# A sum over rows on one core: the block of 17 rows per partition, numbered otherwise

## The chip, the cores and the metric

The kernel runs on one NeuronCore of a Trainium2 chip (trn2). The core has a matrix engine (PE, unused here), a vector engine (DVE), a scalar engine (ACT), a general engine (POOL), a queue engine (SP) that issues transfers, and 16 DMA engines that move data between the chip's memory (HBM) and the core's on-chip memory (SBUF, 128 partitions). The metric is the device time of one execution in microseconds; the median of three runs is given.

## The reference

```python
batch, seq, dim = 32, 512, 1024
x = np.random.randn(batch, seq, dim).astype(np.float32)
divisor = float(dim)

def reference(x, divisor):
    return (np.sum(x, axis=-1) / divisor).astype(np.float32)
```

16,384 rows of 1024 float32 (4 KB a row, 67.1 MB in all) are each summed and divided by 1024. The output is one float32 a row, 64 KB.

## The kernel before

The 16,384 rows are dealt to the 128 partitions, 128 rows (J) to each. They are not one consecutive block a partition but two parts. In the first part, of F = 17 rows per partition, partition p has the rows 17p to 17p + 16: a block of 17 x 4 KB = 68 KB, and the blocks of the 128 partitions follow each other in memory. The second part has W = 111 rows per partition, again one block each (444 KB), of which the first M = 95 are called main and the remaining L = 16 last. The DRAM patterns are `x_first`, `x_main` and `x_last`, and `o_first`, `o_main` and `o_last` for the results.

All loads go through three buffers `bulk0` to `bulk2` of 16 rows per partition, taken in turn. The list `loads` sets their order: 2 rows of the first part (`begin`), then six loads of the main part (five of 16 rows, one of 15), then the other 15 rows of the first part (`first`), then 10 and 4 rows of the last part. The last two rows of a partition come in two small transfers, `pa` (1536 elements) and `pb` (512).

All transfers are issued by SP, in the order in which they stand. The first three loads (line 114) need no wait; they are lifted into the program's first block, ahead of SP's part of the starting barrier, so that they are issued as the very first thing (`start_loads_at_once`). Each later load (line 141) waits until DVE, and where ACT had a share also ACT, has read the load three places before in the same buffer (semaphores `dve` and `act`) and that load has landed. Then SP issues `pa` and `pb` (lines 143, 144), waits for POOL and stores `res` (`o_main`, line 146), waits for POOL again and stores `res0` (`o_first`, line 148), waits for the last sums and stores `fin` (`o_last`, line 205), waits until the two earlier stores have landed, clears the semaphores and waits for the last landing.

DVE takes each load when it has landed. For the loads of the first and main parts it does one `reduce_sum` over all rows of the load that are its own (line 191): for the 2-row load both, for a 16-row load all 16, for the 15-row loads 11 and 9. ACT does the remaining 4 and 6 rows with one activation each that accumulates along the row (line 167). The last part is done row by row, by DVE (line 182, both halves of a row at once) and ACT. POOL scales `res` (line 155) and `res0` (line 159) by 1/1024; the last part is scaled as it is summed.

A transfer of 128 partitions is carried by all 16 DMA engines: in the packet records of the trace each load shows 128 packets, one a partition, and the semaphore that tells of its landing is raised 16 times. SP issues a transfer in some 0.33 to 0.44 us and goes on; the data move on their own.

Of the kernel before, what the change touches and what calls it, by code (L numbers as in the profile page):

```python
# [35 lines left out]
def kernel(  # L36
# [9 lines left out]
    N, D = xf.shape  # L46
    P = nc.NUM_PARTITIONS
    scale = 1.0 / float(divisor)
# [3 lines left out]
    F, L = 17, 16  # L52
    M = J - F - L
    W = M + L
    x_first = bass.AP(tensor=x.tensor, offset=0, ap=[[F * D, P], [D, F], [1, D]])
    x_main = bass.AP(tensor=x.tensor, offset=P * F * D, ap=[[W * D, P], [D, M], [1, D]])
    x_last = bass.AP(tensor=x.tensor, offset=P * F * D + M * D, ap=[[W * D, P], [D, L], [1, D]])
    o_first = bass.AP(tensor=out.tensor, offset=0, ap=[[F, P], [1, F]])
    o_main = bass.AP(tensor=out.tensor, offset=P * F, ap=[[W, P], [1, M]])
    o_last = bass.AP(tensor=out.tensor, offset=P * F + M, ap=[[W, P], [1, L]])  # L60

    def room(name, *shape):
        return nc.alloc_sbuf_tensor(name, [P, *shape], F32).ap()
# [9 lines left out]
    res0 = room("res0", F)  # L73
    res = room("res", M)
    fin = room("fin", L)
# [4 lines left out]
    loads = []  # L80
# [16 lines left out]
    first = [(15, 6)]  # L97
    last = [(10, 4), (4, 1)]
    assert sum(r for r, _ in begin + first) == F
    assert sum(r for r, _ in main) == M and sum(r for r, _ in last) == L - 2  # L100
    for part, src, dst, by in (
        (begin, x_first, res0, 1.0), (main, x_main, res, 1.0),
        (first, x_first[:, 2:], res0[:, 2:], 1.0), (last, x_last, fin, scale),
    ):
        j = 0
        for rows, on_act in part:
            t, s, slot = bulk[n % 3][:, :rows, :], in_bulk[n % 3], n
            n += 1
            loads.append((t, s, src[:, j : j + rows, :], on_act, dst[:, j : j + rows], by, slot))
            j += rows  # L110


# [9 lines left out]
    for k, (t, s, src, on_act, dst, by, slot) in enumerate(loads):  # L122
        rows = t.shape[1]
# [45 lines left out]
    for k, (t, s, src, on_act, dst, by, slot) in enumerate(loads):  # L169
        rows = t.shape[1]  # L170
# [76 lines left out]
```

## Time and profile before

| | |
|---|---|
| median of 3 runs | 160.36 us (160.34 to 160.55) |
| the profiled execution | 160.63 us |
| its span, first to last instruction | 159.3 us |
| DVE busy | 116.5 us (73%), 30 instructions |
| ACT busy | 18.5 us (12%), 33 instructions |
| POOL busy | 1.0 us (1%), 7 instructions |
| DMA | 67.18 MB in 2160 packets, 422 GB/s over the span |

The span is measured between the first and the last instruction; the device time has about 1.3 us more around it. Busy time of an engine does not count register, branch, semaphore and DMA-issuing instructions. The profile is one execution; the median is over other executions, without a profiler.

What each load waits for and when it lands, from the trace's semaphore records and the timeline:

| load | rows | issued at, us | landed at, us |
|---|---|---|---|
| first part (`begin`) | 2 | 0.00 | 4.80 |
| main 1 | 16 | 0.42 | 24.13 |
| main 2 | 16 | 0.89 | 43.52 |
| first part (`first`) | 15 | 99.45 | 137.84 |
| `pa` | 1.5 | 132.01 | 156.65 |
| `pb` | 0.5 | 132.49 | 157.30 |

The difference of a landing and an issue is not the time that a transfer takes alone: the transfers of SP's queue are carried one after the other, and a later one waits for those before it.

### The profile page before, as it was taken

What the parts mean: (1) busy time and instruction counts of PE and PEld (TensorE: products, weight loads), DVE (VectorE), ACT (ScalarE), POOL (GpSimd) and SP (SyncE); (2) the same over time, 40 slices, a digit from 0 to 9 for tenths busy, and PEclk for the clock granted to TensorE, in tenths of its full rate; (3) what the DMA queues carried; (4) which work ended last, traced back from release to release, by engine and by line L of the source; (5) the groups of instructions that cost most, each with busy time, mean ns of one, the idle gap of its engine ahead of it and who ended that gap; (6) DMA issues with size and microseconds to landing.
All of it is one profiled execution on the core that took longest, in us unless ns stands there. A gap on an engine that the chain in (4) does not pass through costs nothing.

```text
span 159.3 us, 140 instructions
## 1 busy us (share of the span) xinstructions
DVE 116.5 (73%) x30; ACT 18.5 (12%) x33; POOL 1.0 (1%) x7
## 2 busy tenths in 40 slices
DVE  0500009999499994999949999499989990399475
ACT  3000000000000000000000000000009100392384
POOL 0000000000000000000000000000000001000000
DMA  9996996996996997999969969988999799797993
GB/s 376 413 527 263 527 527 263 527 510 280 527 510 280 527 477 313 527 395 395 527 263 527 527 263 527 494 386 355 494 494 417 324 494 494 329 483 339 424 425 122
DMA packets 2160, 67.18 MB, mean 422 GB/s; under 512 B 624, under 2 KB 624, under 8 KB 880
## 3 DMA queue, kind: packets, MB, share of 16 engines
q1 hardware_dynamic: 2160, 67.18, 98.0%
HBM read 67.11 MB, written 0.07 MB: 422 GB/s over the span
## 4 chain that ended last, share of the span: by engine, by line
DMA 67%; DVE 29%; another core or an unknown queue 1%; ACT 1%; SPq 1%; issue 0%
DMA bulk<-in_x_dram 52%; DVE res L191 29%; DMA pa<-in_x_dram 15%; ACT junk L167 1%; SPq L114 1%; SPq L141 0%
## 5 line engine op out<-in xcount | busy, mean ns | idle before, releaser
L191 DVE TENSOR_REDUCE res<-bulk 128x16 f32<-128x16384 f32 (+3 forms) x8 | 110.0, 13753 | 37.6 <-DMA bulk<-in_x_dram 37.6
L167 ACT ACTIVATE junk<-bulk 128x1024 f32<-128x1024 f32 x15 | 15.2, 1011 | 136.2 <-DMA bulk<-in_x_dram 136.2
L182 DVE CUSTOM_DVE_ANT_0 bulk<-bulk 128x512 f32<-128x512 f32 x9 | 5.7, 690 | 3.4 <-DMA bulk<-in_x_dram 3.4
L167 ACT ACTIVATION_READ_ACCUMULATOR junk<-bulk 128x1 f32 x15 | 2.8, 187 | 0.0
L167 ACT ACT_TABLE_LOAD x1 | 1.3, 1283 | 2.4 <-PEq L117 2.4
L155 POOL TENSOR_SCALAR res<-res 128x95 f32<-128x95 f32 x1 | 0.5, 463 | 129.2 <-DVE res L191 129.2
L167 ACT ACTIVATE junk<-pa 128x1024 f32<-128x1024 f32 x1 | 1.0, 1027 | 0.7 <-DMA pa<-in_x_dram 0.7
L182 DVE DVE_READ_ACCUMULATOR2_ANT fin<- 128x1 f32 x10 | 0.8, 84 | 0.0
L182 DVE CUSTOM_DVE_ANT_0 pb<-pb 128x257 f32<-128x257 f32 x1 | 0.4, 429 | 0.2 <-DMA pb<-in_x_dram 0.2
L182 DVE CUSTOM_DVE_ANT_0 pa<-pa 128x256 f32<-128x256 f32 x1 | 0.4, 425 | 0.0
L159 POOL TENSOR_SCALAR res<-res 128x17 f32<-128x17 f32 x1 | 0.3, 265 | 15.6 <-DVE res L191 15.6
L167 ACT ACTIVATION_READ_ACCUMULATOR junk<-pa 128x1 f32 x1 | 0.2, 188 | 0.0
L151 POOL MEMSET pb<- 128x2 f32 x1 | 0.1, 100 | 2.0 <-POOLq L117 2.0
L228 POOL MEMSET const-uint8-127<- 128x1 uint8 x1 | 0.1, 102 | 0.0
L228 POOL MEMSET const-bfloat16-1.0<- 128x1 bf16 x1 | 0.1, 101 | 0.0
L228 POOL MEMSET const-float32-0.0<- 128x1 f32 x1 | 0.1, 98 | 0.2 <-issue 0.2
L228 POOL MEMSET const-float32-1.0<- 128x1 f32 x1 | 0.1, 98 | 0.0
L182 DVE DVE_READ_ACCUMULATOR2_ANT pb<- 128x1 f32 x1 | 0.1, 83 | 0.0
## 6 DMA issues: line engine op xcount, KB each, us to landing
bulk<-in_x_dram SPq DMA_DIRECT2D x2, 7680.0 KB, 39.0
bulk<-in_x_dram SPq DMA_DIRECT2D x1, 5120.0 KB, 31.1
bulk<-in_x_dram SPq DMA_DIRECT2D x1, 2048.0 KB, 23.1
bulk<-in_x_dram SPq DMA_DIRECT2D x1, 1024.0 KB, 4.8
pa<-in_x_dram SPq DMA_DIRECT2D x1, 768.0 KB, 24.6
pb<-in_x_dram SPq DMA_DIRECT2D x1, 256.0 KB, 24.8
bulk<-in_x_dram SPq DMA_DIRECT2D x5, 40.8
out_dram<-res SPq DMA_DIRECT2D x1, 47.5 KB, 24.6
```

Source lines behind the costliest of these rows:

```text
L114: i = nc.sync.dma_start(out=t, in_=src).then_inc(s, 16)
L151: nc.gpsimd.memset(pb[:, D - c :], 0.0).then_inc(pool)
L155: nc.gpsimd.tensor_scalar_mul(out=res, in0=res, scalar1=scale).then_inc(pool)
L159: nc.gpsimd.tensor_scalar_mul(out=res0, in0=res0, scalar1=scale).then_inc(pool)
L167: nc.scalar.activation(junk[a % len(junk)], src, COPY, scale=by, accum_out=dst).then_inc(count)
L182: return nc.vector.tensor_tensor_reduce(out=src[:, :h], in0=src[:, :h], in1=src[:, h:], scale=by, scalar=0.0, op0=ADD, op1=ADD, accum_out=dst,
L191: nc.vector.reduce_sum(out=dst[:, :m], in_=t[:, :m, :], axis=AX).then_inc(dve)
L228: nc = _bacc.Bacc("TRN2", target_bir_lowering=False, num_devices=1)
```

## The change

In the first part, partition p = 4a + b (a from 0 to 31, b from 0 to 3) no longer has block p but block a + 32b. The function `spread(step)` gives the two dimensions: 32 steps of one block, and inside each four steps of 32 blocks. `x_first` becomes a function of the first row and the number of rows, which builds the pattern of one load; `o_first` gets the same two dimensions, so that the results go to the rows that belong to the blocks. The list of loads is built with the row offset 2 in place of a slice. Nothing else changes: sizes, buffers, order, waits and the engines' work are as before. In the built program three transfers are touched: the 2-row load, the 15-row load and the store of `res0`; they now have three dimensions a side (32 x 4 x run in DRAM, 128 x 1 x run in SBUF), where all others have two. In the built program every transfer of two dimensions carries a mark named "precooked", and these three no longer do.

```diff
-    x_first = bass.AP(tensor=x.tensor, offset=0, ap=[[F * D, P], [D, F], [1, D]])
+    def spread(step):
+
+        return [[step, P // 4], [P // 4 * step, 4]]
+
+    def x_first(j, rows):
+        return bass.AP(tensor=x.tensor, offset=j * D, ap=[*spread(F * D), [1, rows * D]])
+
     x_main = bass.AP(tensor=x.tensor, offset=P * F * D, ap=[[W * D, P], [D, M], [1, D]])
...
-    o_first = bass.AP(tensor=out.tensor, offset=0, ap=[[F, P], [1, F]])
+    o_first = bass.AP(tensor=out.tensor, offset=0, ap=[*spread(F), [1, F]])
...
-        (first, x_first[:, 2:], res0[:, 2:], 1.0), (last, x_last, fin, scale),
+        (first, x_first, res0, 1.0), (last, x_last, fin, scale),
     ):
-        j = 0
+        j = 2 if part is first else 0
         for rows, on_act in part:
             t, s, slot = bulk[n % 3][:, :rows, :], in_bulk[n % 3], n
             n += 1
-            loads.append((t, s, src[:, j : j + rows, :], on_act, dst[:, j : j + rows], by, slot))
+            loads.append((t, s, src(j, rows) if src is x_first else src[:, j : j + rows, :], on_act, dst[:, j : j + rows], by, slot))
             j += rows
```

## The prediction

> **What bounds the kernel now.** I read four views: the page's DMA lines, the chain of waits in order of time, the groups of instructions, and the start and end of the timeline. First the page's DMA slices and its queue:
>
> ```profile
> DMA  9996996996996997999969969988999799797993
> ...
> q1 hardware_dynamic: 2160, 67.18, 98.0%
> HBM read 67.11 MB, written 0.07 MB: 422 GB/s over the span
> ```
>
> The 16 DMA engines carry 67.18 MB and are at work for 98.0% of the 159.3 us span. The 6s in the row of digits are an effect of where packets of 64 KB begin, not idle time: a packet is booked whole in the slice in which it starts. In the packet records (16 engines; each carries 8 packets of a 128-partition load) the 640 packets of 65,536 B have a median of 2418 ns and a maximum of 2434, and the 256 of 61,440 B have 2267 and 2302. Both are 27.1 B/ns an engine, and the next packet of an engine starts 3 to 4 ns before the one ahead of it ends. So from the first load to the last there is nothing to win or hide: whatever an engine is late by at its start, it is late by at its end.
>
> The chain in order of time (start, length, what) says the same:
>
> ```profile
> 0.00 0.38 SPq L114
> ...
> 0.89 42.63 DMA bulk<-in_x_dram
> ...
> 80.14 39.56 DMA bulk<-in_x_dram
> ...
> 132.01 24.64 DMA pa<-in_x_dram
> ...
> 156.68 1.15 ACT junk L167 x2
> ```
>
> It opens with SP's issue of the first load at L114 and closes with the `pa` transfer, one activation and the last store. The DVE pieces that it names in between are not what limits: the groups show that DVE waited for data before its reductions:
>
> ```profile
> L191 DVE TENSOR_REDUCE res<-bulk 128x16 f32<-128x16384 f32 (+3 forms) x8 | 110.0, 13753 | 37.6 <-DMA bulk<-in_x_dram 37.6
> L167 ACT ACTIVATE junk<-bulk 128x1024 f32<-128x1024 f32 x15 | 15.2, 1011 | 136.2 <-DMA bulk<-in_x_dram 136.2
> ```
>
> Columns: busy us and mean ns of one, then idle us and what ended it. 37.6 us of idle time on DVE, all ended by loads, is slack of the compute side. Last the timeline, its start and end (start, us, what):
>
> ```profile
> 0.00 1.32 SPq L114 DMA_DIRECT2D bulk<-in_x_dram  x3
> ...
> 4.83 2.29 DVE L191 TENSOR_REDUCE res<-bulk 128x2 f32<-128x2048 f32 x1 [4.83 <-DMA bulk<-in_x_dram]
> ...
> 148.06 0.34 SPq L148 DMA_DIRECT2D out_dram<-res  x1
> ...
> 157.85 0.33 SPq L205 DMA_DIRECT2D out_dram<-fin  x1
> ```
>
> Between the first issue and full pace lies the only soft stretch. In the packet records the first of the 128 packets of 8 KB starts at 1.00 us, 0.62 us after the 0.375 us issue has ended. An 8 KB packet at pace takes 309 ns, but most of the first 16 to start take 411 to 816 ns, and one takes 1014. The excess of all 128 over 309 ns, divided by 16, is 0.45 us an engine. The first 64 KB packet starts at 3.92 us on the earliest engine and at 4.53 on the latest; the one next to it starts at 4.25. That spread stays: the last 61,440 B packets start between 134.56 and 135.25, with the second latest at 134.85. The end waits for the latest engine.
>
> **The change part by part.** Three transfers change, all by one pattern: the load of 2 rows (first at L114), the load of 15 rows (at L141, the eighth in the list) and the store of `res0` (L148). Their bytes, order, waits and increments stay, and so do all instructions of DVE, ACT and POOL. What differs is which block of 68 KB a partition gets and that the instruction has three dimensions where it had two: 32 x 4 x run in DRAM, 128 x 1 x run in SBUF. The built program also marks every two-dimensional transfer "precooked" and leaves that mark off these three.
>
> 1. Issue of the first load. L114 holds SP for 375 ns now, and the data start follows it. No row shows an issue with three dimensions. Nearest rows: issues on an otherwise idle SP take 327 to 343 ns, those behind another 424 to 440, all of two dimensions. Lower bound of the extra: 0 (nothing is taken away that would shorten it). Upper bound: one more whole issue, 0.43 us. The record grows by half (three pairs a side for two), which on 375 ns is 0.19; with the lost mark as a second reason I take the middle, 0.21 us. It lies on the path in full: no packet moves before it.
>
> 2. The second and third issue shift by the same 0.21 us. They are hidden: the first load keeps the engines until 3.9 us, and the third issue ends at 1.32. Were that cover gone, it would be the same 0.21 that item 1 counts, not one more.
>
> 3. Issue of the 15-row load. It starts at 99.45 us, and its first packet moves at 100.57 + 8 x 2.267 = 118.7. So 19 us hide even a doubled issue. Behind it on SP are the loads of 10 and 4 rows, which wait for later reductions anyway. Cost 0.
>
> 4. Store of `res0`. Issued at 148.06, landed at 157.67 (last of its 16 semaphore steps), because its 68 B packets (12 ns each) lie behind the loads in the rings. SP waits for it only after the last store's issue at 157.85 has ended at 158.18, and the last store itself lands at 159.27. A longer issue is hidden by the 9.6 us in the ring. The 68 B pieces now go 2,176 B apart where four were adjacent; 1.6 us of cover remain. Cost 0; if all 8 pieces of an engine took ten times 12 ns, 0.96 us, still covered.
>
> 5. The addresses. Neighbouring engines (four partitions each) started 4 x 68 = 272 KB apart and now start 68 KB apart; the four partitions of an engine are 2,176 KB apart where they were 68. At full pace the pitch has not mattered here: the main load (4 x 444 = 1,776 KB between engines) and the 15-row load (272 KB) both run at 27.1 B/ns. For the 15-row load I take 0; the upper bound is that its packets all become like the slowest seen, 8 x (2302 - 2267) = 0.28 us an engine, the lower bound 0, as 2267 is the floor. For the start-up excess I take 0 too, since the rows show no link to the pitch, but both ends are open: below, the latest engine becomes as early as today's earliest, 3.92 - 4.53 = -0.61; above, the excess of 0.45 doubles, +0.45.
>
> One rule speaks to item 5. The Trainium skill, "DMA: Bandwidth & Descriptors", section "Latency and other measured facts", says that a row pitch of 2 MiB between partitions gave 164 GB/s where 512 KiB gave 207, and that a few KiB of padding bring the rate back. Read against this change, 2,176 KB would cost nothing by its padding clause (128 KiB over 2 MiB), and by its first clause 8.9 MB at 164/207 of the pace, an estimate of some 5.5 us more. No row here has such a pitch.
>
> Sum: 0.21 + 0 + 0 + 0 + 0 = +0.21 us. The profiled execution took 160.63 us, 159.30 of it span and 1.33 around it; with the change 159.51 and 160.84. The median of the three runs shown is 160.36, 0.27 under the profiled one, and carries no profiler: 160.36 + 0.21 = 160.57.
>
> **The rivals.** About 0.2% (0.32 us) is what a measurement of this kernel can tell from no change: under 160.04 is faster, over 160.68 slower.
>
> A, the forecast: 160.57. Own range with issue 0 to 0.43 and a start-up that may wander by the 0.28 us between the two latest engines: 160.1 to 161.0.
>
> B, the start-up waits are collisions of engines that begin 272 KB apart, and the new pitch spreads them. For it: the long packets are those at the very start, when all 16 engines begin at equal phases, and they vanish as the engines drift apart. Against it: at the start every engine also has to fill its pipe once, whatever the address. Time: 160.57 - 0.61 = 159.96, faster. It decides if the gain at the latest engine exceeds 0.53 us.
>
> C, the other side: the 68 KB pitch makes them collide more, in the first load and in the 15-row load. Place: the first one or two packets of each engine, and the 61,440 B packets. Price: 0.45 + 0.28 on top of the issue, 160.36 + 0.21 + 0.73 = 161.30, slower; it decides from 0.11 us of loss on top of the issue. For it: the engines now read within 24 blocks, 1.6 MB, where they read over 96; against it: the flat 2267 and 2418 at two very different pitches.
>
> D, the change doesn't do what it says: a transfer with another outermost dimension is dealt to fewer engines. With 8 engines for 16 the first load would take 8 x 0.309 = 2.5 us longer and the 15-row load 8 x 2.267 = 18.1: 181. Against it: 32 divides by 16 as 128 does, and four blocks a step are the four partitions that an engine has.
>
> **How the numbers follow.** A 0.45, B 0.26, C 0.26, D 0.03. A's range lies over three fifths inside the band: same 0.28, slower 0.17. B: faster 0.22, same 0.04. C: slower 0.24, same 0.02. D: slower 0.03. So faster 0.22, same 0.34, slower 0.44. The predicted time is A's, 160.57. The range 159.95 to 161.3 takes in A, B's and C's prices, and leaves out D and the ends beyond them.
>
> **What would show it.** Step 1: the first L114 issue at 0.5 to 0.6 us and the first 8 KB packet at 1.2. Step 5: the first 64 KB packet of the latest engine, 4.74 by A, 4.13 by B, 5.2 by C; the 61,440 B packets at 2267 by A and B, at 2300 or more by C. Steps 3 and 4: DVE's wait before the 15-row reduction and the landing of `res0` unchanged but for the shift. Wrong would make it a pace under 27.1 B/ns, another number of packets, or an issue that is not longer.

## The result and the profile after

The changed kernel takes 161.01 us (median of 6 runs, 160.93 to 161.08) where the kernel before takes 160.44 in runs beside it (6 runs, 160.34 to 160.55): a ratio of 1.0035, 95% interval 1.0022 to 1.0048, or 0.57 us more. Measured again with a later set of kernels it was 161.00 against 160.56, ratio 1.0031 (1.0019 to 1.0042). Differences in us are between medians; the ratios are formed from all runs of both kernels and differ from the quotient of the medians by up to 0.0004. The forecast was 160.57, 0.21 us more, in a range of 159.95 to 161.3.

The page of the changed kernel, its DMA slices and queue:

```profile
DMA  6998989969969969969969979969996999799994
...
q1 hardware_dynamic: 2160, 67.18, 97.8%
HBM read 67.11 MB, written 0.07 MB: 421 GB/s over the span
```

The same 2160 packets and 67.18 MB. The first slice shows 6 for 9, but that is mostly booking: it ends at 4.0 us, and the first 64 KB packet, booked whole where it starts, now comes at 4.43 us instead of 3.92. The page's rates of the first two slices add up to nearly the same, 207 and 581 GB/s for 376 and 413. The rest shows no weaker stretch. The share falls from 98.0% to 97.8% because the span, 159.7 for 159.3 us, has grown at its empty beginning. The chain in order of time (start, length, what):

```profile
0.00 0.67 SPq L120
0.67 0.05 issue
0.71 0.58 SPq L120
...
1.33 42.65 DMA bulk<-in_x_dram
...
80.62 39.43 DMA bulk<-in_x_dram
...
132.37 24.62 DMA pa<-in_x_dram
...
157.01 1.15 ACT junk L173 x2
```

The first issue takes 0.67 us where it took 0.38, the second starts 0.29 us later, and every link behind the issues starts 0.33 to 0.5 us later than its counterpart, with nearly its old length. The second issue, which is of the old form, takes 0.58 where it took 0.42. The groups (busy us and mean ns, then idle us):

```profile
L197 DVE TENSOR_REDUCE res<-bulk 128x16 f32<-128x16384 f32 (+3 forms) x8 | 110.0, 13753 | 38.0 <-DMA bulk<-in_x_dram 38.0
```

And the timeline:

```profile
5.40 2.29 DVE L197 TENSOR_REDUCE res<-bulk 128x2 f32<-128x2048 f32 x1 [5.40 <-DMA bulk<-in_x_dram]
...
148.45 0.62 SPq L154 DMA_DIRECT2D out_dram<-res  x1
158.18 0.35 SPq L211 DMA_DIRECT2D out_dram<-fin  x1
```

DVE's work is the same 110.0 us; it waits 0.4 us longer in all, and its first wait ends at 5.40 for 4.83. The store of `res0` takes 0.62 us to issue for 0.34. The packet records say where the stream begins, for all kernels of this study. Each row is one profiled execution; the last column is the time of the timed runs as a ratio to the kernel before in the same set. The records carry no engine number: as a 64 KB packet takes 2.4 us and the first sixteen start within 0.9 us of each other, the sixteenth to start is taken as the latest engine's first.

| kernel | first issue, us | first packet, us | latest engine's first 64 KB packet, us | ratio and 95% interval |
|---|---|---|---|---|
| before | 0.38 | 1.00 | 4.53 | |
| after | 0.67 | 1.44 | 5.05 | 1.0035 (1.0022 to 1.0048) |
| after, measured again | 0.65 | 1.45 | 5.02 | 1.0031 (1.0019 to 1.0042) |
| begin_only | 0.61 | 1.40 | 5.07 | 1.0023 (1.0013 to 1.0033) |
| form_old_place | 0.64 | 1.41 | 4.97 | 1.0036 (1.0023 to 1.0050) |
| plain_first | 0.55 | 1.33 | 4.87 | 1.0018 (1.0009 to 1.0027) |
| plain_three | 0.55 | 1.34 | 4.85 | 1.0021 (1.0013 to 1.0030) |
| rest_only | 0.38 | 1.02 | 4.62 | 1.0001 (0.9990 to 1.0013) |
| main_start | 0.38 | 1.02 | 4.49 | 0.9994 (0.9985 to 1.0003) |
| place_two_dim | 0.38 | 1.01 | 4.69 | 1.0019 (1.0010 to 1.0029) |
| the same again | 0.39 | 1.04 | 4.68 | 1.0012 (1.0003 to 1.0021) |
| extra_issue | 0.38 + 0.41 | 1.47 (of the opening load) | 5.05 | 1.0043 (1.0031 to 1.0056) |

(begin4 and begin1 are left out: their opening load has another size.)

### The profile page after: what moved, and what is told of

Its sections match the earlier page's. It is cut to its first block, busy times and chain, and to the rows that moved or that the text cites. A ratio compares the mean times of both kernels' runs of the same rounds, so it can differ in the third digit from the quotient of the medians.

```text
span 159.7 us, 140 instructions
## 1 busy us (share of the span) xinstructions
DVE 116.5 (73%) x30; ACT 18.5 (12%) x33; POOL 1.0 (1%) x7
## 2 busy tenths in 40 slices
DMA packets 2160, 67.18 MB, mean 421 GB/s; under 512 B 624, under 2 KB 624, under 8 KB 880
## 3 DMA queue, kind: packets, MB, share of 16 engines
q1 hardware_dynamic: 2160, 67.18, 97.8%
## 4 chain that ended last, share of the span: by engine, by line
DMA 67%; DVE 29%; another core or an unknown queue 1%; SPq 1%; ACT 1%; issue 0%
DMA bulk<-in_x_dram 51%; DVE res L197 29%; DMA pa<-in_x_dram 15%; SPq L120 1%; ACT junk L173 1%; SPq L147 0%
```

## The experiments

Theory: the opening load's issue is longer in the new form, and everything after it is late by that. Rival: the new addresses collide at the start or later. Both predict a loss in the first 5 us, so the form and the place were separated.

**begin_only: the opening load alone**

```diff
+    x_begin = bass.AP(tensor=x.tensor, offset=0, ap=[[F * D, P // 4], [P // 4 * F * D, 4], [1, 2 * D]])
...
+            loads.append((t, s, x_begin if part is begin else src[:, j : j + rows, :], on_act, dst[:, j : j + rows], by, slot))
```

> Only the 2-row load at the start gets the new pattern; the 15-row load and the store of res0 are as before, so the first two rows of a partition belong to other blocks than their results say. If the whole loss of 0.57 us is made in the first load (my theory, by its issue or by its addresses): +0.5 to +0.6 us over before, first issue about 665 ns. If the 15-row load or the store carries part of it: clearly less, +0.2 to +0.4.

Measured: 160.95 us against 160.59, +0.36, ratio 1.0023 (1.0013 to 1.0033). Its chain:

```profile
0.00 0.61 SPq L115
...
1.28 42.79 DMA bulk<-in_x_dram
```

The issue is 0.61 us. The median lies in the second expectation, that the rest carries part of the loss; the interval, +0.21 to +0.53 us, reaches into the first as well. So what the rest does had to be measured by itself.

**rest_only: everything but the opening load**

```diff
+            loads.append((t, s, x_old[:, :2, :] if part is begin else src(j, rows) if src is x_first else src[:, j : j + rows, :], on_act, dst[:, j : j + rows], by, slot))
```

> The other half: the 15-row load and the store have the new pattern, the 2-row load is as before, so again two rows of each partition are summed for the wrong block. My theory: 0 (within 0.1 us of before), since the longer issues lie 19 us and 9.6 us ahead of need. The rival that the 15-row load reads slower at the new pitch: +0.1 to +0.3, with 61,440 B packets above 2267 ns.

Measured: 160.62 against 160.59, ratio 1.0001 (0.9990 to 1.0013). From its chain:

```profile
0.00 0.38 SPq L121
...
0.91 42.67 DMA bulk<-in_x_dram
```

And from its timeline:

```profile
148.14 0.62 SPq L155 DMA_DIRECT2D out_dram<-res  x1
157.87 0.34 SPq L212 DMA_DIRECT2D out_dram<-fin  x1
```

The store's issue takes 0.62 us here as in the changed kernel, and the last store starts at 157.87, where before it was 157.85. The long issue is there, and neither it nor the 15-row load with its new pattern shows a cost: the 61,440 B packets keep their median of 2267 ns, and the interval of the time runs from -0.16 to +0.21 us. The loss that can be seen is in the opening load.

**plain_first: the form without the place.** The opening load stays two-dimensional and where it was; only the mark is taken off.

```diff
-    for t, s, src, *_ in loads[:3]:
+    for n, (t, s, src, *_) in enumerate(loads[:3]):
+        nc.dge_precook = n > 0
```

> The kernel before, with the mark precooked taken off the first load alone: two dimensions, old addresses. Theory of the form (the unmarked issue makes the loss): first issue 0.55 to 0.67 us, first packet at about 1.4 us, +0.4 to +0.57 us in all. Theory of the addresses: +0.2 to +0.3 us at most, the length of the issue alone, and the start-up excess of an engine stays at 0.45 us instead of 0.55.

Measured: 160.88 against 160.59, +0.29, ratio 1.0018 (1.0009 to 1.0027). In the chain:

```profile
0.00 0.55 SPq L115
...
0.60 0.57 SPq L115
...
1.21 42.63 DMA bulk<-in_x_dram
```

The first packet moves at 1.33, near the 1.4 of the theory of the form, but the time came out below its range and inside the +0.2 to +0.3 of the theory of the addresses, and the start-up excess of this profile, 0.50 us, lies between the two. By itself this run does not decide. Without the mark the issue is 0.17 us longer, but the first packet is 0.33 us later: the gap between the end of the issue and the first packet grows from 0.62 to 0.78 as well. The mark alone makes half of the loss of 0.57 us, or two thirds of the 0.44 measured again.

**place_two_dim: the place without the form**

```diff
+    x_begin = bass.AP(tensor=x.tensor, offset=0, ap=[[F * D // 4, P], [1, 2 * D]])
```

> The opposite: the first load keeps two dimensions and the mark, but its partitions lie 17 KB apart, so that neighbouring engines begin 68 KB apart as in the changed kernel (the rows read are the wrong ones for the first two results of a partition). Theory of the form: 0 within 0.15 us, first issue 375 ns, first packet at 1.0 us. Theory of the addresses: +0.2 to +0.4 us with a start-up excess of 0.55 us or more. If the old pitch had collided, the gain I gave a quarter: -0.2 to -0.5.

Measured: 160.83 against 160.59, +0.24, ratio 1.0019 (1.0010 to 1.0029); in a repeat 160.83 against 160.60, ratio 1.0012 (1.0003 to 1.0021). The theory of the form had no more than 0.15. Its repeat was expected thus:

> The two-dimensional marked opening load with partitions 17 KB apart once more, since its first measurement (+0.24 us) came without a later start in its profile. If that place costs time at the start: +0.15 to +0.3 us again and a first 64 KB packet of the latest engine after 4.7 us. If it was the packets of one slow engine later on, as in its first profile (one 64 KB packet of 2598 ns): within 0.15 us of before.

The latest engine's first 64 KB packet is at 4.69 and 4.68, 0.06 to 0.2 behind the other marked kernels with 8 KB opening packets (4.49 to 4.62). So a place can cost, some 0.2 us, and with 17 KB between partitions this one does. That it costs it at the start is likely but not shown: the two times lie just under the 4.7 that the expectation asked for, and rest_only, which lost nothing, has 4.62. And it is not the changed kernel's place: groups of four partitions start 68 KB apart in both, but inside a group the partitions are 17 KB apart here and 2,176 KB there. That left the rival open.

**form_old_place: three dimensions at the old place**

```diff
+    x_begin = bass.AP(tensor=x.tensor, offset=0, ap=[[4 * F * D, P // 4], [F * D + 32, 4], [1, 2 * D]])
```

> The first load gets three dimensions as in the changed kernel, but stays where it was: 32 steps of 272 KB and four of 68 KB plus 128 B, so that the two inner steps cannot be merged (the first two results of a partition are sums of shifted rows). Theory of the form: issue 0.61 to 0.67 us and +0.33 to +0.45 us, the same as with only the first load renumbered. Theory of the addresses: the two-dimensional unmarked load gave +0.29, so +0.29 to +0.33 here, and a start-up excess of 0.45 to 0.50 us an engine rather than 0.55 to 0.68.

Measured: 161.10 against 160.56, +0.54, ratio 1.0036 (1.0023 to 1.0050), and the changed kernel in the same set:

> The changed kernel once more, beside the other kernels of this set on one chip, to have its loss against the same runs of before. If the first load carries everything: +0.3 to +0.45 us, as the kernel with only that load changed gave +0.36. If something of the rest adds to it: +0.55 us again, as in the first measurement.

161.00, +0.44, ratio 1.0031 (1.0019 to 1.0042), in the first of the two ranges, with an interval that takes in the second. The three-dimensional load at the old place came out above both of its ranges. The chain of the form at the old place:

```profile
0.00 0.64 SPq L115
...
1.30 42.60 DMA bulk<-in_x_dram
```

With the old addresses (but for the 128 B), and the new form, the loss is as large as the whole change's. The rival of the addresses falls: the new place costs nothing that can be seen beside the form. What the form does beyond the late first packet stays open: the start-up excess is 0.50 to 0.75 us in the six profiles with an unmarked opening load and 0.45 to 0.61 in the five with a marked one of 8 KB and nothing ahead of it, so the form may slow the first packets a little too, but the ranges overlap. Whether the kernel with only its opening load changed (+0.36) really loses less than these two can't be told, as the intervals overlap.

**plain_three: is only the first issue on the path?** The mark is taken off the first three loads.

> The kernel before with the mark taken off the first three loads instead of the first alone. If only the issue that comes first lies on the path: +0.29 us, the same as with the mark off the first load. If each issue costs on the path: +0.5 us or more.

Measured: 160.87 against 160.56, +0.31, ratio 1.0021 (1.0013 to 1.0030), as with the mark off the first alone (+0.29). In the chain the second issue takes 0.58 us; the third takes 0.60 in its record.

```profile
0.00 0.55 SPq L115
...
0.61 0.58 SPq L115
...
1.23 42.58 DMA bulk<-in_x_dram
```

The second and third issue are hidden.

**extra_issue: another way to be late.** A small load of 64 B a partition is issued ahead of the opening load.

```diff
+    i = nc.sync.dma_start(out=spare, in_=x_main[:, 0, :16]).then_inc(in_spare, 16)
...
-    for s in (out_first, out_main):
+    for s in (out_first, out_main, in_spare):
```

> The kernel before with one more small marked load (64 B a partition, into a spare buffer) issued ahead of the first. It delays the first load's issue by about 0.42 us. If the delay of the first load goes through to the end one to one: +0.4 to +0.45 us. If the small load fills the engines' pipes, so that the start-up excess of 0.45 us becomes smaller: +0.1 to +0.3 us or even 0.

Measured: 161.29 against 160.56, +0.73, ratio 1.0043 (1.0031 to 1.0056), more than either expectation. Its chain:

```profile
0.00 0.38 SPq L115
...
0.43 0.41 SPq L118
...
0.89 0.43 SPq L118
```

All issues are short here, and none has lost its mark; still the lateness goes through. That a late start costs at least its own length is borne out, though barely: the interval is +0.50 to +0.90 us, and the opening load's first packet is late by 0.47. The 0.26 us by which the median exceeds that are not explained. The profile of this kernel, 161.15 us, does not show them: the latest engine's first 64 KB packet is late by 0.53 and the span longer by 0.5. Besides the delay, the edit adds the small load's own 128 packets, its semaphore steps and a wait near the end for a landing that came at 1.74 us.

**main_start: the numbering kept, the start freed of it.** F becomes 15, the opening 2 rows come from the main part, and the new pattern serves only the 15-row load and the store.

```diff
-    F, L = 17, 16
+    F, L = 15, 16
...
-        (begin, x_first, res0, 1.0), (main, x_main, res, 1.0),
-        (first, x_first[:, 2:], res0[:, 2:], 1.0), (last, x_last, fin, scale),
+        (begin, x_main, res, 1.0), (main, x_main, res, 1.0),
+        (first, x_first, res0, 1.0), (last, x_last, fin, scale),
     ):
-        j = 0
+        j = 2 if part is main else 0
```

> The new numbering kept, but the start freed of it: the first part has 15 rows (F = 15, blocks of 60 KB) and is loaded at once by the eighth load, with the new pattern; the opening 2-row load takes rows of the main part, two dimensions, marked, partitions 452 KB apart. Theory of the form: within 0.15 us of before, first issue 375 ns, first packet at 1.0 us. If the new numbering itself costs anything: +0.2 us or more. If the opening load's place matters (452 KB instead of 68): a shift either way of 0.2 us or more with the first packet still at 1.0 us.

Measured: 160.55 against 160.60, ratio 0.9994 (0.9985 to 1.0003): no loss. Its timeline has the old start and, for one of its seven later loads, the long issue (0.65 us in the records of that line):

```profile
0.00 1.34 SPq L120 DMA_DIRECT2D bulk<-in_x_dram  x3
...
4.85 2.29 DVE L197 TENSOR_REDUCE res<-bulk 128x2 f32<-128x2048 f32 x1 [4.85 <-DMA bulk<-in_x_dram]
```

DVE starts at 4.85, as before the change (4.83), for 5.40 with it. With blocks of 60 KB the renumbered partitions lie 1,920 KB apart here; rest_only had the 2,176 KB of the change. So the numbering is free as far as these two can tell (intervals -0.24 to +0.05 and -0.16 to +0.21 us), and the form of the first issue is what costs.

**begin4 and begin1: what are the slow first packets?** The opening load gets 4 rows or 1.

```diff
-    begin = [(2, 0)]
+    begin = [(4, 0)]
...
-    first = [(15, 6)]
+    first = [(13, 5)]
```

> The kernel before with 4 rows instead of 2 in the opening load and 13 in the later one. If the slow first packets wait a time of their own (latency): an excess near 0.45 to 0.7 us an engine as with 8 KB packets, and 0 within 0.15 us. If the excess is by bytes (the memory is slow at first): an excess well above 0.7, and slower.

> The same the other way: 1 row in the opening load (4 KB packets), 16 in the later one. By latency: the same excess an engine and 0 within 0.15 us. By bytes: an excess near half, and -0.1 to -0.3 us. DVE has 37 us of slack, so its order of work should not matter in either.

Measured: 160.76 (ratio 1.0006, 0.9995 to 1.0018) and 160.68 (1.0007, 0.9998 to 1.0017) against 160.60: no difference that is clear. The excess over a packet at pace, summed and divided by 16, is 0.55 us an engine with 16 KB packets and 0.38 with 4 KB, where 8 KB gave 0.45 to 0.61 in the marked kernels. A fourfold size changes it by under half, in one profile each: it reads as mostly a time of its own, not a slow pace. Neither size wins.

## Why the prediction was right, and where it was off

1. The bound. Right: pace and packet numbers are unchanged (medians 2418 and 2267 ns), and the lateness of the start reaches the end. How fully it does is less clear: in the two profiles the latest engine's first 64 KB packet came 0.53 us later, but the last 61,440 B packet (135.62 for 135.25) and the end of the span only 0.35 to 0.37 later; there the kernel before had one engine 0.40 us behind all others (135.25, the next 134.85), and the changed kernel has none. The timed medians differ by 0.57, and by 0.44 when measured again; that 0.53 and 0.57 are so near is partly chance.

2. Issue of the first load, +0.21. Right as the place of the loss; the size was under half of the measured one. The record grew by 0.29 us (0.38 to 0.67), inside the stated 0 to 0.43, but past the sign of 0.5 to 0.6 for the record, as the first packet at 1.44 was past the sign of 1.2. But the price is not the record: the first packet moved by 0.44, because the gap behind the issue also grew, from 0.62 to 0.78. Of the 0.44 the lost mark makes 0.33 (plain_first) and the third dimension 0.06 to 0.11, by the first packets of the three-dimensional kernels. The forecast had given the larger role to the dimensions, by halves of a record; the mark is the larger one. In the timed runs the mark makes 0.29 to 0.31 us; that the third dimension adds to it fits the medians (+0.36 to +0.57), but their intervals overlap.

3. The second and third issue, 0: right (plain_three). The prediction left out that the second would be longer too (0.58 for 0.42); it is hidden as well.

4. The 15-row load's issue and the store, 0 each: right (rest_only, main_start). The cover named is there: the 15-row load is issued at 99.92 and its first packet moves at 119.25, 19 us later. DVE's wait before its 15-row reduction is 6.29 us for 6.26, as the sign asked. The store landed at 158.28 and the last store at 159.62, so 1.3 us of cover were left.

5. The addresses, 0 with both ends open: right as a whole (form_old_place), and for the 15-row load nearly to the packet: 2267 ns in the median and 2311 at most, and the packets of an engine took 18.18 us in sum, in the mean, before and after. The rule of the Trainium skill quoted there ("DMA: Bandwidth & Descriptors", "Latency and other measured facts") is not contradicted in its padding clause: 2,176 KB between partitions cost nothing here. It is no test of the rule, though, as only runs of four partitions lie at that pitch, and the page's figures are of copies between HBM tensors. The item counts four partitions to an engine; the 128 packets of a load on 16 engines make eight. That a place can matter in the opening load was shown by another one, with 17 KB.

The rivals, and luck: A's own range stood as 160.1 to 161.0, and the measured 161.01 lies just above it (its terms, 160.36 + 0.43 + 0.28, add up to 161.07, so its upper end was added up too low). The whole range held the result with room to spare only because C's price had widened it. By the prediction's own bounds 160.57 was no difference and 161.01 is slower. B (spreading gains) found nothing for it, no marked start was faster than before beyond its interval. C's time, 161.30, was nearer to the measured 161.01 than A's 160.57, though its mechanism was not at work (form_old_place), and its sign, the latest engine's first 64 KB packet at 5.2, would have been read into the 5.05 of the changed kernel. That sign was badly chosen, since it lumps a late issue with slow packets; the first packet's start, at 1.44, told them apart. D fell with the time, which is nowhere near 181, and with the 15-row load, whose packets and landing (138.23 for 137.84) are late only by the start.

## What to carry to other kernels

In a stream whose DMA engines never idle, the time to the first packet is a price that nothing hides; keep the very first transfer in the plainest form (here two dimensions, with the mark in the built program), and put patterns of more dimensions into transfers that are issued while others are still running. The same pattern cost 0.36 us in the first transfer alone (0.44 to 0.57 with the whole change) and nothing that could be measured in the eighth. Judge an issue by the start of its first packet, not by the length of its record.

## What the runs showed of the hardware

- An unmarked issue delays also the one behind it: the second, marked issue takes 0.57 to 0.58 us after an unmarked first and 0.42 to 0.43 after a marked one.
- The start-up excess of an engine wanders between executions: 0.55 us in one profile of the changed kernel, 0.75 in another, 0.45 and 0.50 in two kernels with the same opening load. A single profile can't settle a difference of 0.1 us there.
- One small transfer ahead of a full stream cost 0.73 us in the median (interval 0.50 to 0.90), more than the 0.47 by which it delayed the stream's first packet. Why stays open.
